# Attention scores of a hybrid decoder on Trainium2: one product over 128 rows in place of two heads side by side on 64 rows

## The chip, the core and the metric

The kernel runs on one core of one Trainium2 chip, as one launch. The metric is the device time of one launch in microseconds. The core has a matrix engine (PE, with its weight loads shown as PEld), a vector engine (DVE), a scalar engine (ACT), a general engine (POOL) and a queue engine (SP) that issues nearly all transfers. Each engine works through its own instructions in the order in which they stand, and waits on semaphores for the others.

## What is computed

The reference is a decoder trunk of two layers on 512 tokens of width 1024: the first layer mixes tokens by forgetting attention with 16 heads of 64, the second by a short gated convolution, and each is followed by a squared-ReLU MLP and a gated embedding. The change is in the attention of the first layer, whose core is:

```python
q = q * HEAD_DIM ** -0.5                       # 16 heads of 64
c = cumsum(log_sigmoid(f_logit))               # per head and token
s = einsum('bhqd,bhkd->bhqk', qb, k)           # per block of 128 queries
s = s + cb[..., :, None] - c[..., None, :]
s = where(k_pos <= q_pos, s, NEG_INF)
pr = softmax(s)
o = einsum('bhqk,bhkd->bhqd', pr, v)
return o @ w_out
```

All arrays are float32. The kernel multiplies in a rounded float32 form (fp32r in the profile): each operand is split into a high part, which is the rounded value, and a low part, which is the rest, and a product is made of three: high by high, low by high, high by low.

## The kernel before, in words

**Stages.** `attention` (L336) norms the tokens, projects the values (tiles `v`), and then runs three kinds of work interleaved. `project(i)` (L418) makes q and k of the two heads 2i and 2i+1 as one 128-row page each: rows 0 to 63 belong to the first head, rows 64 to 127 to the second. It takes 48 products of 512 columns (tiles `qk`, L214 to L216), first for k, then for q, and a split into high (ACT, L222 and L432) and low (DVE, L223 and L433) after each. `scores(i, b)` (L459) multiplies query block b of both heads with the keys up to that block, in tiles `sc`, and does the softmax on DVE (L474, L479), ACT (L478) and POOL (L480), on pages `prr`, `pr` and `prl` into which `bias(h)` (L441) has loaded the decay terms (`neg_c`) by four transfers for each head. `turn(h, j)` (L484) transposes the weights (tiles `pT`) and splits them into `ph` and `pl`; `mix(h, j)` (L498) multiplies them with the values (tiles `ps_o`).

**The products of the scores.** For one block the kernel issues three products for each head (L466 to L470): q.hi by k.hi, q.hi by k.lo and q.lo by k.hi. Each contracts over the 64 rows of one head. The two heads' products alternate in the text of the program; a scheduler may move them apart.

**The order of the work.** A loop over steps c (L611) places the interleaved work: scores run 12 steps ahead of `turn` (`SCORED`), `mix` runs 2 behind it (`LAG`), and a generator `stream` (L548) supplies filler for PE: first the steps of `project(1)` to `project(7)`, three products each, 112 steps in all, then parts of the output projection (tiles `o`). A number of steps, `share + AHEAD`, says how many filler steps are done by step c (L615 to L621); `AHEAD` is 2. The tile framework's scheduler then moves instructions within that order. Weights arrive by transfers into 14 `raw` pages (L119), are split into `wh` (ACT, L222) and `wl` (DVE, L223), and everything else lives on 70 pages of 128 by 512. All of the kernel's loads, the decay terms and the weights among them, are issued by SP in one order.

Of the kernel before, what the change touches and what calls it, by code (L numbers as in the profile page):

```python
# [8 lines left out]
F32 = mybir.dt.float32  # L9
# [16 lines left out]
PUT_OFF = 46000  # L26
LAG = 2
AHEAD = 2
PAGES = 70
RAWS = 14  # L30
LEAD = 1
# [32 lines left out]
def trunk(ctx: ExitStack, tc, x, pT, g, wv, wqk, bf, wo, wci, cw, wco, wup, wdn, wpp, wpg, out):  # L64
# [13 lines left out]
    def bank(name):  # L78
        return psum.tile([P, S], F32, tag="ps", name=name)
# [256 lines left out]
    def attention(hT, first_x, g0, by_hand):  # L336
# [78 lines left out]

        stacked, probs, outs, both = {}, {}, {}, {}

        def project(i):  # L418

            q, key = (Pair(page(f"{n}h{i}", F32R), page(f"{n}l{i}", F32R)) for n in "qk")  # L420
            stacked[i] = q, key
            for s in (1, 0):
                ps = bank(f"qk{i}_{s}")
                for k in range(KT):
                    mm3(
                        ps, narrow("qk", i, k=k, c=s * P),
                        hT.at(lambda h: h[:, k, :]), k == 0, k == KT - 1,
                    )
                    if k < KT - 1:
                        yield  # L430
                if s == 0:
                    nc.scalar.mul(q.hi[:, :S], ps, HD**-0.5)  # L432
                    nc.vector.scalar_tensor_tensor(  # L433
                        out=q.lo[:, :S], in0=ps, scalar=HD**-0.5, in1=q.hi[:, :S].bitcast(F32),
                        op0=ALU.mult, op1=ALU.subtract,
                    )
# [22 lines left out]
        def scores(i, b):  # L459


            q, key = stacked[i]
            n = (b + 1) * P
            nm = max(n, 256)
            heads = [(2 * i + e, slice(64 * e, 64 * e + 64), bank(f"sc{2 * i + e}_{b}")) for e in range(2)]
            for s, (at, to) in enumerate(((q.hi, key.hi), (q.hi, key.lo), (q.lo, key.hi))):  # L466
                for _, r, ps in heads:
                    nc.tensor.matmul(  # L468
                        ps[:, :nm], at[r, b * P : n], to[r, :nm], start=s == 0, stop=s == 2
                    )  # L470
            for h, _, ps in heads:
# [139 lines left out]
        for c in range(-SCORED, n_sc + LAG):  # L611
# [350 lines left out]
```

## Time and profile before

| | |
|---|---|
| median of 3 runs | 1263.35 us (1263.23 to 1263.46) |
| span of the profiled execution, first to last instruction | 1262.1 us |
| PE busy in the span | 1238.7 us (98%) |
| DVE, ACT, POOL busy | 906.1, 604.0, 627.5 us |
| stretch with scores in it | 82.0 to 227.6 us |

The profiled execution has no time of its own beside its span, so the span stands for it: it lies 1.25 us under the median. In rows of the timeline, the columns are start, duration, engine, line, operation, output and inputs, and the number of instructions merged into the row; two heads' products that start together are merged as x2. Matmuls are pipelined and their ends modelled, so what one product costs is read from the distance between two starts and not from its duration. In rows of windows, each engine has its busy microseconds and its instructions. A stage is read from its own window: the share over the whole span mixes stages.

### The profile page before, as it was taken

The numbers are of one execution on the slowest core, as the hardware profiler recorded it, in microseconds if no ns is written. First come the engines' busy times: TensorE is split into PE (matmuls) and PEld (weight loads), VectorE is DVE, ScalarE is ACT, GpSimd is POOL, SyncE is SP. The second block draws the span as 40 slices with busy tenths as digits, with TensorE's granted clock in tenths as the row PEclk, the third lists the DMA queues.
The fourth block names the chain that finished last, engine by engine and source line by source line (L and its number), as shares of the span: only waits on it lengthen the run. The fifth ranks groups of instructions, "written<-read, shape, count | busy, mean of one in ns | idle before, by whom it ended". The sixth has DMA issues, their size and how long they took to land.

```text
span 1262.1 us, 18000 instructions
## 1 busy us (share of the span) xinstructions
PE 1238.7 (98%) x6036; PEld 1022.3 (81%) x6036; DVE 906.1 (72%) x1386; ACT 604.0 (48%) x1293; POOL 627.5 (50%) x631
## 2 busy tenths in 40 slices
PE   7999999999999999999999999999999999999997
PEld 6877777788888888888789988889788888888876
DVE  5645666767788788879867444457778897779973
ACT  5445656654645434554455333344653445535451
POOL 2027555328787777876211000016777777878210
PEclk9999999999999999999999999999999999999999
DMA  7554342161432244227333233432323442235401
GB/s 249 152 142 149 100 126 76 62 224 65 134 95 86 87 134 134 84 68 258 126 100 94 74 101 101 141 124 86 94 74 101 134 130 84 71 117 175 159 18 50
DMA packets 83228, 144.48 MB, mean 114 GB/s; under 512 B 9600, under 2 KB 16816, under 8 KB 83136
## 3 DMA queue, kind: packets, MB, share of 16 engines
q1 hardware_dynamic: 82928, 143.07, 36.3%
q8 instruction: 47, 0.77, 0.2%
q14 instruction: 45, 0.37, 0.1%
q10 hardware_dynamic: 144, 0.26, 0.1%
q0 software_dynamic: 64, 0.00, 0.0%
HBM read 136.93 MB, written 6.37 MB: 114 GB/s over the span
## 4 chain that ended last, share of the span: by engine, by line
PE 60%; DVE 18%; POOL 7%; issue 6%; ACT 6%; DMA 3%; SPq 1%; DVEq 0%; POOLq 0%; ACTq 0%
DVE wl L223 10%; POOL s L720 4%; PE up L215 3%; PE up L216 3%; PE up L214 3%; ACT wh L222 3%; PE dn L215 3%; PE qk L214 3%; PE dn L216 3%; PE dn L214 3%; DVE acc L752 2%; PE qk L216 2%; PE qk L215 2%; PE sc L468 2%; PE pg L214 2%
## 5 line engine op out<-in xcount | busy, mean ns | idle before, releaser
L223 DVE TENSOR_TENSOR wl<-raw,wh 128x512 fp32r<-128x512 f32 (+1 forms) x404 | 365.2, 955 | 25.3 <-ACT wh L222 24.6
L222 ACT CAST wh<-raw 128x512 fp32r<-128x512 f32 (+1 forms) x404 | 219.5, 619 | 8.9 <-DVE xd L296 5.0
L215 PE MATMUL up<-hTh,wl 128*128 128x512 f32 (+1 forms) x576 | 210.5, 366 | 0.0
L216 PE MATMUL up<-hTl,wh 128*128 128x512 f32 (+1 forms) x576 | 210.0, 366 | 0.0
L214 PE MATMUL up<-hTh,wh 128*128 128x512 f32 (+1 forms) x576 | 209.7, 366 | 0.0
L223 POOL TENSOR_TENSOR wl<-T,wh 128x512 fp32r<-128x512 f32 x112 | 160.9, 1468 | 35.8 <-ACT wh L222 32.0
L215 PEld LDWEIGHTS up<-hTh,wl 128*128 128x128 f32 x576 | 108.7, 189 | 17.6
L214 PEld LDWEIGHTS up<-hTh,wh 128*128 128x128 f32 x576 | 108.6, 189 | 17.5
L216 PEld LDWEIGHTS up<-hTl,wh 128*128 128x128 f32 x576 | 108.3, 189 | 17.3
L752 DVE TENSOR_TENSOR acc<-dn,acc 128x512 f32<-128x512 f32 x168 | 107.4, 679 | 10.5 <-PE dn L216 10.5
L131 POOL TENSOR_TENSOR T<-raw,raw 128x512 f32<-128x512 f32 x56 | 87.5, 1573 | 37.0 <-DMA raw<-in_wdn 24.8
L706 ACT ACTIVATE r<-up 128x512 f32<-128x512 f32 (+1 forms) x72 | 38.7, 547 | 126.3 <-PE up L216 126.3
L131 POOL TENSOR_TENSOR T<-raw,T 128x512 f32<-128x512 f32 x56 | 91.3, 1631 | 2.2
L692 DVE TENSOR_TENSOR q<-r 128x512 f32<-128x512 f32 (+1 forms) x72 | 66.9, 936 | 29.2 <-ACT r L706 29.2
L237 POOL TENSOR_SCALAR cor_r_v<-cos,cos 128x1 f32<-128x1 f32 x4 | 1.6, 398 | 159.1 <-ACT junk L245 159.1
L222 ACT CAST wh<-T 128x512 fp32r<-128x512 f32 x112 | 61.2, 617 | 0.0
L222 ACT CAST A11h<-q 128x256 fp32r<-128x256 f32 x28 | 11.4, 407 | 99.9 <-DVE q L692 99.9
L214 PE MATMUL pg<-wh,hTh 128*128 128x512 f32 x128 | 50.9, 398 | 3.4 <-ACT hTh L222 3.3
L214 PE MATMUL qk<-hTh,wh 128*128 128x512 f32 x128 | 53.0, 414 | 0.0
L759 POOL TENSOR_TENSOR acc<-acc,acc 128x512 f32<-128x512 f32 x28 | 47.0, 1708 | 10.0 <-DVE acc L752 10.0
L216 PE MATMUL qk<-hTl,wh 128*128 128x512 f32 x128 | 50.8, 397 | 0.0
L215 PE MATMUL qk<-hTh,wl 128*128 128x512 f32 x128 | 50.5, 395 | 0.0
(236 smaller groups left out, 3067.1 us busy)
## 6 DMA issues: line engine op xcount, KB each, us to landing
raw<-in_wup SPq DMA_DIRECT2D x128, 256.0 KB, 2.9
raw<-in_wdn SPq DMA_DIRECT2D x128, 256.0 KB, 2.8
raw<-in_wci SPq DMA_DIRECT2D x48, 256.0 KB, 3.5
raw<-in_wqk SPq DMA_DIRECT2D x32, 256.0 KB, 3.8
raw<-in_wpg SPq DMA_DIRECT2D x32, 256.0 KB, 3.8
g<-in_g SPq DMA_DIRECT2D x22, 256.0 KB, 5.4
prl<-neg_c SPq DMA_DIRECT2D x16, 256.0 KB, 6.7
raw<-in_wo SPq DMA_DIRECT2D x16, 256.0 KB, 2.7
```

The costliest lines, as they stand in the source:

```text
L131: nc.gpsimd.tensor_tensor(out=B[name, p], in0=B[a, p], in1=B[b, p], op=ALU.subtract)
L214: nc.tensor.matmul(ps, a.hi, b.hi, start=start, stop=False)
L215: nc.tensor.matmul(ps, a.lo, b.hi, start=False, stop=False)
L216: nc.tensor.matmul(ps, a.hi, b.lo, start=False, stop=stop)
L222: nc.scalar.copy(hi, src)
L223: eng.tensor_tensor(out=lo, in0=src, in1=hi.bitcast(F32), op=ALU.subtract)
L468: nc.tensor.matmul(ps[:, :nm], at[r, b * P : n], to[r, :nm], start=s == 0, stop=s == 2)
L692: nc.vector.tensor_tensor(out=out, in0=r, in1=r, op=ALU.mult)
L706: nc.scalar.activation(r[:, :n], ps[:, :n], AF.Relu)
L720: sums = lambda out, a, b, op: nc.gpsimd.tensor_tensor(out=out, in0=a, in1=b, op=op)
L752: nc.vector.tensor_tensor(out=a, in0=banks[s], in1=a, op=ALU.add)
L759: nc.gpsimd.tensor_tensor(out=a, in0=a, in1=acc[i, s][:, :S], op=ALU.add)
```

## The change

Each head gets its high and low parts one above the other, so that one product over 128 rows sums two of the three. For the first head of a pair, the rows of q.hi become (high of q, low of q) and a new page pair `k0` holds (high of k, high of k) and (low of k, low of k); for the second head a new page `q1` holds (high of q, low of q), and the old k pages become (high, high) and (low, low). The new sum also holds low by low, which the three products left out. Getting there takes nine transfers inside SBUF for each pair of heads, each of 64 rows by 512, issued by SP (`place`): six after the split of k and three after that of q. Some overwrite rows that an earlier one of them reads, and wait for it. `scores` then issues two products for each head, over all 128 rows, in place of three over 64. Three more pages are held for each pair. The filler is done sooner: `STACK` lets `project` run 12 steps ahead of `share` and not 2, until its 112 steps are done; the output projection's steps keep the old rule.

```diff
+STACK = 12
...
+        def place(out, to, src, of):
+            nc.sync.dma_start(out[to, :S].bitcast(F32), src[of, :S].bitcast(F32))
...
-            stacked[i] = q, key
+            low, high = slice(0, HD), slice(HD, P)
...
+                    q1 = page(f"q1_{i}", F32R)
+                    place(q1, low, q.hi, high)
+                    place(q1, high, q.lo, high)
+                    place(q.hi, high, q.lo, low)
                 else:
                     split(key.hi[:, :S], key.lo[:, :S], ps)
+                    k0 = Pair(*(page(f"k0{s}{i}", F32R) for s in "hl"))
+                    for of, to in ((key.hi, k0.hi), (key.lo, k0.lo)):
+                        place(to, low, of, low)
+                        place(to, high, of, low)
+                        place(of, low, of, high)
                 yield
+            stacked[i] = (q.hi, k0), (q1, key)
...
-            heads = [(2 * i + e, slice(64 * e, 64 * e + 64), bank(f"sc{2 * i + e}_{b}")) for e in range(2)]
-            for s, (at, to) in enumerate(((q.hi, key.hi), (q.hi, key.lo), (q.lo, key.hi))):
-                for _, r, ps in heads:
+            heads = [(2 * i + e, bank(f"sc{2 * i + e}_{b}")) for e in range(2)]
+            for (h, ps), (at, key) in zip(heads, stacked[i]):
+                for s, to in enumerate((key.hi, key.lo)):
                     nc.tensor.matmul(
-                        ps[:, :nm], at[r, b * P : n], to[r, :nm], start=s == 0, stop=s == 2
+                        ps[:, :nm], at[:, b * P : n], to[:, :nm], start=s == 0, stop=s == 1
                     )
...
-            while done < share + AHEAD:
+            while done < max(share + AHEAD, min(share + STACK, 112)):
```

PE's order, at block 2 of heads 8 and 9 (`sc8_2`, `sc9_2`), before; `qh`, `ql`, `kh` and `kl` are the high and low parts of q and k, and each score product is one head's, over 64 rows:

```order
L468 MATMUL sc8_2_2176<-kh4_1686,qh4_1684 128x384
L468 MATMUL sc8_2_2176<-kl4_1687,qh4_1684 128x384
L468 MATMUL sc8_2_2176<-kh4_1686,ql4_1685 128x384
L216 MATMUL qk5_0_2142<-hTl_84,wh42_1460 128x512
L214 MATMUL qk5_0_2142<-hTh_83,wh42_1460 128x512
L215 MATMUL qk5_0_2142<-hTh_83,wl42_1461 128x512
L216 MATMUL qk5_0_2142<-hTl_84,wh42_1460 128x512
L214 MATMUL qk5_0_2142<-hTh_83,wh43_1504 128x512
L468 MATMUL sc9_2_2177<-kh4_1686,qh4_1684 128x384
L468 MATMUL sc9_2_2177<-kl4_1687,qh4_1684 128x384
L509 MATMUL ps_o5_2117<-ph5_2_2113,v2_1_141 128x256
L468 MATMUL sc9_2_2177<-kh4_1686,ql4_1685 128x384
```

The same block now; `k0h`, `k0l` and `q1` are the new pages, and each product is over 128 rows:

```order
L482 MATMUL sc8_2_2267<-k0h4_1719,qh4_1575 128x384
L482 MATMUL sc8_2_2267<-k0l4_1720,qh4_1575 128x384
L217 MATMUL qk6_1_2179<-hTl_84,wh47_1705 128x512
L482 MATMUL sc9_2_2268<-kh4_1577,q1_4_1839 128x384
L482 MATMUL sc9_2_2268<-kl4_1578,q1_4_1839 128x384
L523 MATMUL ps_o5_2199<-ph5_2_2195,v2_1_141 128x256
L524 MATMUL ps_o5_2199<-pl5_2_2196,v2_1_141 128x256
```

The scheduler had moved the two heads' products apart in both; there were six over 64 rows, and there are four over 128. In the whole program the score products stood in 45 stretches between other work and now stand in 41.

PE's order around block 1 of heads 12 and 13 (`sc12_1`, `sc13_1`), before:

```order
L487 MATMUL pT9_2_2702<-ident_75,prr9_1903 128x128
L487 MATMUL pT9_2_2702<-ident_75,prl9_1902 128x128
L509 MATMUL ps_o9_2709<-ph9_0_2616,v0_2_134 128x512
L510 MATMUL ps_o9_2709<-pl9_0_2617,v0_2_134 128x512
L468 MATMUL sc12_1_2712<-kh6_2278,qh6_2276 128x256
L468 MATMUL sc12_1_2712<-kl6_2279,qh6_2276 128x256
L468 MATMUL sc13_1_2713<-kh6_2278,qh6_2276 128x256
L468 MATMUL sc13_1_2713<-kl6_2279,qh6_2276 128x256
L468 MATMUL sc12_1_2712<-kh6_2278,ql6_2277 128x256
L468 MATMUL sc13_1_2713<-kh6_2278,ql6_2277 128x256
L214 MATMUL qk7_0_2734<-hTh_83,wh48_1985 128x512
L215 MATMUL qk7_0_2734<-hTh_83,wl48_1986 128x512
```

And now, at the same place:

```order
L501 MATMUL pT9_2_2775<-ident_75,prr9_1988 128x128
L501 MATMUL pT9_2_2775<-ident_75,prl9_1987 128x128
L524 MATMUL ps_o8_2654<-pl8_3_2687,v3_2_146 128x256
L523 MATMUL ps_o9_2782<-ph9_0_2705,v0_2_134 128x512
L524 MATMUL ps_o9_2782<-pl9_0_2706,v0_2_134 128x512
L482 MATMUL sc12_1_2785<-k0h6_2319,qh6_2175 128x256
L482 MATMUL sc12_1_2785<-k0l6_2320,qh6_2175 128x256
L523 MATMUL ps_o9_2782<-ph9_1_2747,v1_2_138 128x384
L482 MATMUL sc13_1_2786<-kh6_2177,q1_6_2439 128x256
L482 MATMUL sc13_1_2786<-kl6_2178,q1_6_2439 128x256
L501 MATMUL pT9_3_2805<-ident_75,prl9_1987 128x128
L524 MATMUL ps_o9_2782<-pl9_1_2748,v1_2_138 128x384
```

The filler (`qk7`) has left this place. Between the first transpose of head 9 (`pT9_0`) and the first product of the output projection (`o0_0`) there stood 36 filler products of 512 columns; now there is none, since they stand earlier.

SP's order of transfers at the second pair of heads, before; `raw` are weights, `prr`, `pr` and `prl` the decay terms of a head:

```order
L119 DMA raw48_1987<-in_wqk 128x512
L119 DMA raw49_2009<-in_wqk 128x512
L453 DMA prr2_1025<-neg_c_151 128x128
L453 DMA pr1_1023<-neg_c_151 128x256
L453 DMA prr2_1025<-neg_c_151 128x384
L453 DMA prl2_1024<-neg_c_151 128x512
L453 DMA prr3_1100<-neg_c_151 128x128
L453 DMA pr1_1023<-neg_c_151 128x256
L453 DMA prr3_1100<-neg_c_151 128x384
L453 DMA prl3_1099<-neg_c_151 128x512
L119 DMA raw50_2054<-in_wqk 128x512
L453 DMA prr4_1218<-neg_c_151 128x128
```

And now, at the same place:

```order
L421 DMA k0h1_1013<-kh1_960 64x512 x2
L421 DMA k0l1_1014<-kl1_961 64x512 x2
L421 DMA kh1_960<-kh1_960 64x512
L421 DMA kl1_961<-kl1_961 64x512
L421 DMA q1_1_1068<-qh1_958 64x512
L468 DMA prr2_1074<-neg_c_151 128x128
L421 DMA q1_1_1068<-ql1_959 64x512
L421 DMA qh1_958<-ql1_959 64x512
L468 DMA pr1_1072<-neg_c_151 128x256
L468 DMA prr2_1074<-neg_c_151 128x384
L468 DMA prl2_1073<-neg_c_151 128x512
L468 DMA pr1_1072<-neg_c_151 128x256
```

The nine transfers of a pair stand ahead of the decay terms of the next heads (`prr2`, `pr1`, `prl2`), and some of each follow one another in one queue.

More of the change, by code (lines that the diff above doesn't have):

```diff
@@ L459, in scores @@
         def scores(i, b):
-            q, key = stacked[i]
             n = (b + 1) * P
             nm = max(n, 256)
-            heads = [(2 * i + e, slice(64 * e, 64 * e + 64), bank(f"sc{2 * i + e}_{b}")) for e in range(2)]
-            for s, (at, to) in enumerate(((q.hi, key.hi), (q.hi, key.lo), (q.lo, key.hi))):
-                for _, r, ps in heads:
+            heads = [(2 * i + e, bank(f"sc{2 * i + e}_{b}")) for e in range(2)]
+            for (h, ps), (at, key) in zip(heads, stacked[i]):
+                for s, to in enumerate((key.hi, key.lo)):
                     nc.tensor.matmul(
-                        ps[:, :nm], at[r, b * P : n], to[r, :nm], start=s == 0, stop=s == 2
+                        ps[:, :nm], at[:, b * P : n], to[:, :nm], start=s == 0, stop=s == 1
                     )
-            for h, _, ps in heads:
+            for h, ps in heads:
                 pr = probs[h][b]
```

## The prediction

> **What bounds the kernel now.** I read the page first, then the waits of PE, the chain, and the windows and timeline of the stretch with scores.
>
> ```profile
> span 1262.1 us, 18000 instructions
> PE 1238.7 (98%) x6036; PEld 1022.3 (81%) x6036; DVE 906.1 (72%) x1386; ACT 604.0 (48%) x1293; POOL 627.5 (50%) x631
> ```
>
> PE is busy 98% of the span, the next engine 72%. In the windows of the attention (columns: stretch, its length, then busy us and instructions of PE, PEld, DVE, ACT, POOL, the clock, and transfers) PE is never idle until 227 us, at full clock:
>
> ```profile
> 82.00:194.20 112.20, 112.20 (x581) 82.92 (x581) 71.60 (x221) 67.98 (x174) 67.41 (x113) 1.00 0.42 122
> 194.20:212.10 17.90, 17.90 (x94) 13.00 (x92) 12.40 (x36) 12.53 (x32) 11.33 (x20) 1.00 0.38 128
> 212.10:217.00 4.90, 4.90 (x24) 4.05 (x24) 2.84 (x8) 1.94 (x6) 3.13 (x2) 1.00 0.01 3
> 217.00:227.00 10.00, 10.00 (x59) 7.50 (x58) 6.24 (x22) 5.85 (x17) 3.49 (x7) 1.00 0.00 0
> 227.00:232.00 5.00, 4.91 (x29) 3.65 (x30) 4.90 (x13) 4.74 (x13) 2.37 (x3) 1.00 0.17 60
> 232.00:238.00 6.00, 6.00 (x28) 4.57 (x27) 4.79 (x12) 3.71 (x10) 4.28 (x9) 1.00 0.35 119
> ```
>
> But a busy PE is not one that streams without gaps. The timeline of PE at one block of 512 keys, both heads together:
>
> ```profile
> 89.00 0.39 PE L215 MATMUL qk<-hTh,wl 128*128 128x512 f32 x1
> 89.22 0.39 PE L216 MATMUL qk<-hTl,wh 128*128 128x512 f32 x1
> 89.54 0.50 PE L468 MATMUL sc<-kh,qh 64*128 64x512 f32 x2
> 89.88 0.40 PE L468 MATMUL sc<-kl,qh 64*128 64x512 f32 x2
> 90.11 0.39 PE L468 MATMUL sc<-kh,ql 64*128 64x512 f32 x2
> 90.44 0.50 PE L214 MATMUL qk<-hTh,wh 128*128 128x512 f32 x1
> 90.77 0.40 PE L215 MATMUL qk<-hTh,wl 128*128 128x512 f32 x1
> ```
>
> A product of 512 columns takes 0.23 us from start to start (about 0.2275 over a long run), and two heads on 64 rows each share one slot. From 89.22 to 90.77 there are five slots, 1.14 us, and 1.55 us pass. So 0.41 us are lost at one visit to the 64-row form: 0.09 ahead of the first score product, and 0.10 to 0.11 behind it, behind the last and behind the first product after. A block whose heads stand apart pays that twice, and its slots hold one head each:
>
> ```profile
> 121.54 0.39 PE L215 MATMUL qk<-hTh,wl 128*128 128x512 f32 x1
> 121.86 0.44 PE L468 MATMUL sc<-kh,qh 64*128 64x384 f32 x1
> 122.14 0.33 PE L468 MATMUL sc<-kl,qh 64*128 64x384 f32 x1
> 122.31 0.34 PE L468 MATMUL sc<-kh,ql 64*128 64x384 f32 x1
> 122.58 0.50 PE L216 MATMUL qk<-hTl,wh 128*128 128x512 f32 x1
> 122.92 0.40 PE L214 MATMUL qk<-hTh,wh 128*128 128x512 f32 x1
> ```
>
> Here 1.38 us pass for two slots of 0.2275 and three of 0.17: again 0.41 lost. A different operand alone costs nothing: among 128-row products the trace goes from `qk` to `ps_o` and back at the usual distances, 0.23 and 0.17:
>
> ```profile
> 130.01 0.40 PE L216 MATMUL qk<-hTl,wh 128*128 128x512 f32 x1
> 130.24 0.34 PE L509 MATMUL ps_o<-ph,v 128*128 128x384 f32 x1
> 130.41 0.39 PE L214 MATMUL qk<-hTh,wh 128*128 128x512 f32 x1
> ```
>
> The loss belongs to the change of row form. The Trainium skill, page TensorEngine Tiling (Array Packing), section Key Properties, says the same: a change of tiling mode drains the engine. It gives no price; the rows above do.
>
> **The change, part by part.** *Visits removed.* By the order the 192 score products stand in 45 stretches between other work. At 0.41 us each that is 18.5 us; the total would be less only if some visit were free, and none in the timeline is, so I hold 17 to 20 us possible and take 19.
>
> *Slots.* Blocks by width, from the counts of one of the three products, of which each block has two:
>
> ```profile
> L468 PE MATMUL sc<-kh,qh x64: 275/411/502, 82.0 to 227.0; 64*128 64x256 f32 x32, 64*128 64x384 f32 x16, 64*128 64x512 f32 x16
> ```
>
> That is 16 blocks of 256, 8 of 384, 8 of 512. The price of 256 columns over 128 rows is 0.12 us:
>
> ```profile
> 62.11 0.28 PE L215 MATMUL v<-wh,hTl 128*128 128x256 f32 x1
> 62.23 0.28 PE L216 MATMUL v<-wl,hTh 128*128 128x256 f32 x1
> 62.35 0.28 PE L214 MATMUL v<-wh,hTh 128*128 128x256 f32 x1
> ```
>
> Now each block takes four slots: 64 x 0.12 + 32 x 0.17 + 32 x 0.2275 = 20.4 us. Before, a block took three slots with its heads together and six with them apart; by the timeline 14, 2 and 6 blocks of the three widths are together, one of 256 takes four slots and the rest six, so 52 x 0.115 + 42 x 0.17 + 30 x 0.2275 = 19.9 us. The slots cost 0.5 us more. PE's work falls by 19 - 0.5 = 18.5 us.
>
> At this point a rule speaks against the change. The Trainium skill, the same page, section Theoretical Speedup, gives a contraction of at most 64 rows up to twice the speed by two row tiles at once, which the change gives up. By that rule alone, with all 32 blocks together and no visit paid, the kernel would become 5 us slower (a fourth slot for each block, 16 x 0.12 + 8 x 0.17 + 8 x 0.23). The x2 rows agree with it for the slots, and the 0.41 us beside them is what it leaves out.
>
> *Filler moved.* The 36 filler products that stood between `pT9_0` and `o0_0` (8.2 us) now stand earlier; PE's work in sum is the same. Their cover is gone from the stretch 194.2 to 212.1. PE's own work left there is 17.9 - 8.2 - 2.5 (six visits) = 7.2 us, and DVE has 12.4 us there now. If all of DVE's work stayed there and bound, PE would lose 5.2 us; if the scores, which run 12 steps ahead, and the weight splits that leave with the filler free enough of DVE, nothing. By the new order two weight splits, some 1.4 us, leave the stretch, and the output projection's first products follow to absorb a rest. I take 2.5, between the ends.
>
> *The thinner tail.* From 217 to 238 six visits and some slots go, about 2.7 us, of 21. DVE is busy 15.9 us there, but 4.90 of 5.00 between 227 and 232, where a faster PE finds it late. Bounds 0 and 2.7 us lost; I take 1, since 217 to 227 has room (6.2 us of DVE in what would be 7.7).
>
> *Transfers.* 72 are added, nine for each pair, of 64 rows by 2 KB, 128 KB each. No row shows one inside SBUF. The nearest are (issue, count, size, median us from issue to landing):
>
> ```profile
> raw<-in_wqk SPq DMA_DIRECT2D x32, 256.0 KB, 3.8
> prl<-neg_c SPq DMA_DIRECT2D x16, 256.0 KB, 6.7
> pr<-neg_c SPq DMA_DIRECT2D x16, 128.0 KB, 5.9
> kept<-xb SPq DMA_DIRECT2D x8, 256.0 KB, 2.2
> ```
>
> A copy out of SBUF lands in 2.2 us at twice the size, decay terms in 5.9 to 6.7 because ten are issued at once. I take 2.5, and 6.7 as the upper end. The last step of a pair is two landings deep: `q1` must land before the rows of `qh` under it are overwritten. Before that come the last product and the split of q:
>
> ```profile
> 126.82 0.40 PE L216 MATMUL qk<-hTl,wh 128*128 128x512 f32 x1
> 127.58 0.60 ACT L432 ACTIVATE qh<-qk 128x512 fp32r<-128x512 f32 x1
> 128.31 0.69 DVE L433 SCALAR_TENSOR_TENSOR ql<-qk,qh 128x512 fp32r<-128x512 f32 x1
> ```
>
> From the product's start to the end of the split: 2.2 us. So a pair is ready after 2.2 + 2 x 2.5, some 7.5 us with issue. By the order, PE has this much other work between the last product of q and the first score: 9.7 us at the first pair, 11.7 at the second, 14.8 at the third, 18 at the next four, 12 at the last. The step `STACK` buys that, and the transfers are covered by projection products. What is queued behind a waiting transfer on SP: the next decay terms, for which POOL and then DVE wait, and weights, which are split two pairs ahead of use. Three more pages per pair also make some `k0` wait for a page that PE frees some 3 us later. I charge 0.5 us, with ends at 0 and, from the longer landing, 18 us (second rival). A gain from the transfers themselves is excluded: nothing waited for less.
>
> Sum: 18.5 - 2.5 - 1 - 0.5 = 14.5 us. The other stages keep their order and PE bounds them, so the gain should stay. The span of 1262.1 becomes 1247.6, and the time, which lies 1.25 us over the span, 1248.9.
>
> **The rivals.** *First: DVE takes over in both thin stretches.* Everything at its upper end, 5.2 and 2.7 us, and waits from `pT` through ACT and DVE to `ps_o` at each of the six steps without filler, 0.6 us each, would leave 18.5 - 5.2 - 2.7 - 3.6 = 7 us: 1256.4. For it: 4.90 of 5.00. Against: 71.6 of 112.2 before. Chance 0.11.
>
> *Second: the transfers land late.* At 6.7 us each a pair is ready after 2.2 + 13.4 + about 1 for issue, 16.6 us, and the scores wait 6.9, 4.9, 1.8 and 4.6 us at the first, second, third and last pair, 18.2 in all: 18.5 - 18.2 - 3.5 is 3.2 us slower, 1266.6. At 5.9 each the waits are 5.3, 3.3, 0.2 and 3.0, and 3.2 us are gained, 1260.2. Its middle is 1263. It begins at landings of 3.3 us. For it: ten decay terms share the queue. Against it: the new transfers stand ahead of them. Chance 0.08: 0.03 faster, 0.03 within the measurement, 0.02 slower.
>
> *Third, on the other side: the loss is not the row form's.* If the 0.41 us belongs to each new run of scores (their accumulation begins, their weights load anew), it stays at the 41 stretches that the order now has. Four fewer save 1.6 us, the slots cost 0.5 and the other losses 4: 2.9 us slower, 1266.3. It decides where a visit still costs more than 0.34 us (18.5 - 41 x 0.34 = 4.5). Against it: 0.23 and 0.17 around `ps_o`, which also begins accumulations with new weights. Chance 0.06.
>
> **How the numbers follow.** The forecast, with losses between nothing and 8 us, has 0.75: gains of 10 to 19 us. The predicted time is 1248.9. The range takes in the first rival and all of the visits: 1243.5 to 1256.4, and leaves out the other two and a little of the forecast's ends. A measurement of this kernel can tell 0.2%, 2.5 us, from no change. Faster: 0.75 + 0.11 + 0.03 = 0.89; same 0.03; slower 0.06 + 0.02 = 0.08.
>
> **What would show it right or wrong.** In the profile after, score rows should read 128x256 to 128x512 and stand 0.12, 0.17 and 0.23 us apart, with no row of `qk` late behind them; a distance of 0.3 there means the third rival. The waits of PE should show `sc` or `qk` behind transfers for under 1 us in sum; several us at the first two pairs are the second. Between `pT9_0` and `o0_0` waits of `ps_o` for `pl` of some 2.5 us are expected; over 5, with DVE full, are the first. The prediction is wrong if PE's time from the first score to the last falls by less than 10 us.

## The result: slower, 1278.49 us against 1263.29

| kernel | median us | range us | ratio to the kernel before, 95% interval |
|---|---|---|---|
| before | 1263.29 | 1263.18 to 1263.46 | |
| changed | 1278.49 | 1275.94 to 1280.22 | 1.0118 [1.0106, 1.0130] |

The change costs 15.2 us where 14.5 were to be gained. The profiled execution took 1278.0 us, its span is 1276.3.

```profile
span 1276.3 us, 18024 instructions
PE 1230.1 (96%) x5972; PEld 1028.0 (81%) x5972; DVE 906.2 (71%) x1386; ACT 602.2 (47%) x1293; POOL 631.1 (49%) x631
```

PE's busy time has fallen by 8.6 us, from 1238.7, and its idle time has risen from 23.4 us (1262.1 - 1238.7) to 46.2. Nearly all of that lies in the attention: the windows from the first score product to the last product of `ps_o` (columns as in the prediction), before and after:

```profile
82.00:247.00 165.00, 164.23 (x855) 122.51 (x855) 108.39 (x321) 101.82 (x259) 92.02 (x152) 1.00 0.35 105
```

```profile
85.00:260.00 175.00, 152.42 (x773) 126.36 (x772) 104.88 (x320) 98.00 (x256) 93.61 (x152) 0.94 0.49 142
```

PE is busy 12 us less in this stage, 4 of them because some 18 filler products now stand ahead of it, and stands idle for 22.6 us where it stood for 0.8. The granted clock is 0.94 in place of 1.00, and the DMA engines are busy 0.49 of the time in place of 0.35. What PE waits for is nearly one thing, by the waits of PE (total, times, longest):

```profile
PE ps_o L523 <- POOL ph L508: 20.8, 7, 7.6
```

`ph` at L508 is the short zero fill of a probability page, 0.2 us of POOL's work. PE's timeline shows the new score products, and then the longest such wait:

```profile
113.01 0.39 PE L482 MATMUL sc<-k0h,qh 128*128 128x512 f32 x1
113.24 0.39 PE L482 MATMUL sc<-k0l,qh 128*128 128x512 f32 x1
113.46 0.39 PE L482 MATMUL sc<-kh,q 128*128 128x512 f32 x1
113.69 0.39 PE L482 MATMUL sc<-kl,q 128*128 128x512 f32 x1
113.92 0.39 PE L217 MATMUL qk<-hTl,wh 128*128 128x512 f32 x1
...
116.91 0.27 PE L501 MATMUL pT<-ident,prl 128*128 128x128 f32 x1
124.82 0.58 PE L523 MATMUL ps_o<-ph,v 128*128 128x256 f32 x1 [7.64 <-POOL ph L508]
125.20 0.41 PE L524 MATMUL ps_o<-pl,v 128*128 128x256 f32 x1
125.41 0.63 PE L215 MATMUL qk<-hTh,wh 128*128 128x512 f32 x1
125.84 0.63 PE L216 MATMUL qk<-hTh,wl 128*128 128x512 f32 x1
```

The scores and the `qk` behind them stand 0.23 us apart: the loss at each visit is gone, as forecast. Behind the wait products of 512 columns stand 0.43 us apart, and do so until 129.9.

Why the fill is late is read one engine back. POOL's timeline of the same time:

```profile
115.36 0.29 POOL L469 TENSOR_SCALAR_AFFINE_SELECT pr<-pr 128x128 f32<-128x128 f32 x1 [2.74 <-DMA pr<-neg_c]
...
118.94 0.29 POOL L469 TENSOR_SCALAR_AFFINE_SELECT prl<-prl 128x128 f32<-128x128 f32 x1 [1.51 <-DMA prl<-neg_c]
...
123.10 0.29 POOL L469 TENSOR_SCALAR_AFFINE_SELECT prr<-prr 128x128 f32<-128x128 f32 x1 [0.86 <-DMA prr<-neg_c]
124.33 0.29 POOL L469 TENSOR_SCALAR_AFFINE_SELECT prl<-prl 128x128 f32<-128x128 f32 x1 [0.93 <-DMA prl<-neg_c]
124.56 0.21 POOL L508 MEMSET ph<- 128x128 f32 x1
```

POOL works its row in order, and the fill stands behind masks (L469) of the next pair's decay terms, whose loads have not landed. From 80 to 250 us POOL waits 60.8 us for such loads at its masks; before it was 24.9. One step further back is SP, which issues those loads. Its timeline before:

```profile
93.87 0.38 SPq L453 DMA_DIRECT2D prr<-neg_c  x1
...
99.52 1.92 SPq L453 DMA_DIRECT2D prr<-neg_c  x2
101.53 0.38 SPq L453 DMA_DIRECT2D prl<-neg_c  x1
```

And after, the same two heads' decay terms (scores began 3 us later here):

```profile
98.29 1.35 SPq L421 DMA_DIRECT2D k0h<-kh  x2
99.75 1.17 SPq L421 DMA_DIRECT2D k0l<-kl  x2
105.56 0.46 SPq L421 DMA_DIRECT2D kh<-kh  x1
...
107.90 0.58 SPq L468 DMA_DIRECT2D prr<-neg_c  x1
108.53 0.46 SPq L421 DMA_DIRECT2D q<-ql  x1
111.06 0.46 SPq L421 DMA_DIRECT2D qh<-ql  x1
...
114.73 1.96 SPq L468 DMA_DIRECT2D prr<-neg_c  x2
116.78 0.38 SPq L468 DMA_DIRECT2D prl<-neg_c  x1
```

The decay terms are issued at 107.90 and 114.73 instead of 93.87 and 99.52. Ahead of them and among them SP issues nine transfers at about half a microsecond each, and stands still twice: from 100.9 to 105.56 until the two copies out of `kh` have landed, which the transfer into `kh` would overwrite, and from 109.0 to 111.06 likewise for q. SP's waits from 80 to 250 us (total, times, longest), and the landings from 70 to 250:

```profile
SPq L421 <- DMA k0h<-kh: 22.6, 7, 4.7
SPq L421 <- DMA q<-qh: 9.3, 7, 2.2
```

```profile
k0h<-kh SPq DMA_DIRECT2D x16, 128.0 KB, 6.1
q<-qh SPq DMA_DIRECT2D x8, 128.0 KB, 2.3
```

The copies of q land in 2.3 us. The copies out of k into `k0`, issued behind loads, take 6.1 and 5.1. The decay terms are issued late and do not land late: from issue to landing they take 4.9 to 7.0 us (median of each size), before 5.0 to 6.7.

### The profile page after: what moved, and what is told of

It is laid out like the page before. It is cut to its first block, busy times and chain, and to the rows that moved or that the text cites. A ratio compares the mean times of both kernels' runs of the same rounds, so it can differ in the third digit from the quotient of the medians.

```text
span 1276.3 us, 18024 instructions
## 1 busy us (share of the span) xinstructions
PE 1230.1 (96%) x5972; PEld 1028.0 (81%) x5972; DVE 906.2 (71%) x1386; ACT 602.2 (47%) x1293; POOL 631.1 (49%) x631
## 4 chain that ended last, share of the span: by engine, by line
PE 69%; DVE 12%; DMA 5%; issue 4%; ACT 4%; POOL 4%; SPq 1%; DVEq 0%; POOLq 0%; ACTq 0%
PE up L217 6%; PE up L216 6%; PE up L215 6%; DVE wl L224 5%; PE dn L216 5%; PE dn L215 5%; PE dn L217 5%; PE pg L215 2%; PE pg L217 2%; PE pg L216 2%; PE qk L215 2%; PE qk L216 2%; PE qk L217 2%; ACT junk L246 2%; DVE n_h L254 1%
## 5 line engine op out<-in xcount | busy, mean ns | idle before, releaser
L469 POOL TENSOR_SCALAR_AFFINE_SELECT prr<-prr 128x128 f32<-128x128 f32 x32 | 11.1, 352 | 82.0 <-DMA prr<-neg_c 48.6
```

## The experiments

Three theories were on record first. **Theory 1:** SP waits for landings at the overwriting transfers, so that decay terms are issued late; POOL stands at their masks, its zero fills come late, and PE's `ps_o` waits. **Theory 2:** the added bytes make every transfer land late, whoever waits. **Theory 3:** the stretch left without filler by `STACK` is what costs the time. All times are medians beside 1263.3 to 1263.6 for the kernel before in the same sets of runs. Where a run leaves the stacking out of the result, so that its output is not the reference's, its entry says so.

### The terms of the forecast, apart

**No transfers.** The 128-row products read q's and k's pages as they are, so the stacking is left out of the result:

```diff
-                    q1 = page(f"q1_{i}", F32R)
-                    place(q1, low, q.hi, high)
...
-            stacked[i] = (q.hi, k0), (q1, key)
+            stacked[i] = (q.hi, key), (q.hi, key)
```

> The 128-row products and the earlier filler stay; the nine transfers and the three new pages of each pair are left out, so both heads multiply the pages as they are and the scores of the two heads are summed. Theory 1 (SP waits for landings of transfers that overwrite rows, issues the next decay terms late, and POOL's masks and the memsets behind them hold up ps_o) and theory 2 (the added bytes make everything land late) both say that the 34 us of gaps on PE go: 1244 to 1250 us, with no wait of ps_o for POOL over 0.5 us. Theory 3 (the stretch without filler costs the time) says over 1255 us, with gaps behind pT9.

Measured 1249.09 us, ratio 0.9887 [0.9872, 0.9902]. The window of the stage:

```profile
85.00:231.00 146.00, 144.01 (x774) 121.36 (x773) 107.41 (x320) 97.55 (x256) 92.11 (x152) 1.00 0.38 114
```

PE is idle for 2 us here, and for 22.6 in the changed kernel. Products, tail and earlier filler together come out at 14.2 us of gain; so the nine transfers, with the three pages that they fill, cost 1278.49 - 1249.09 = 29.4 us. Theory 3 is out.

**Earlier filler alone**, in the kernel before:

```diff
+STACK = 12
...
-            while done < share + AHEAD:
+            while done < max(share + AHEAD, min(share + STACK, 112)):
```

> The kernel before with the rule for the earlier filler alone (STACK = 12), old products, no transfers. Theories 1 and 2: 1263 to 1267 us, since DVE works while PE has no filler. Theory 3: over 1272 us.

Measured 1268.85, ratio 1.0044 [1.0027, 1.0061]: 5.5 us. That isn't the price of the missing filler alone, since the order of the old products changed with it. PE's timeline shows 49 visits to the 64-row form in place of 45, and more heads apart. Counted from the starts, with the prediction's prices for 256, 384 and 512 columns, the visits lose 20.1 us in place of 18.5 and the score products' slots take 23.2 in place of 19.9: 4.9 of the 5.5 us. So 1268.85 - 1249.09 = 19.8 us isn't what the products gain over the kernel before. The same count for the run without transfers gives 1.1 us lost around its 43 stretches of scores and 20.1 in slots. By PE's rows the products thus gain 18.5 + 19.9 - 1.1 - 20.1 = 17.2 us over the kernel before, and 3.0 of them are lost again to the moved filler and the tail, which leaves the 14.2.

**The transfers and the filler with the old products** (64 rows, six to a block; the transfers' results go unused or overwrite halves that the products read, so the result is not the reference's):

```diff
-            stacked[i] = (q.hi, k0), (q1, key)
+            stacked[i] = q, key
...
```

> The transfers and the earlier filler stay; the products are the old ones, three for each head over 64 rows, on pages that the transfers have partly overwritten, so the scores differ. Theories 1 and 2: the visits to the 64-row form come back and the gaps stay, so 1278.5 + 19 = 1290 to 1299 us if both costs are separate; less, down to 1280, if the slower PE gives the transfers time. Theory 3: about 1264 us.

Measured 1277.38, ratio 1.0108 [1.0093, 1.0123], less than expected, and the same as the changed kernel. With nine transfers some 17 us or more of PE's work make no difference: PE no longer sets the pace of this stage.

### What of the transfers costs

**Six instead of nine**, those that overwrite left out (so the pages keep halves of their own there, and the scores are not the reference's):

```diff
-                    place(q.hi, high, q.lo, low)
...
-                        place(of, low, of, high)
```

> Of the nine transfers the three that overwrite rows read by an earlier one (kh, kl and qh onto themselves or from ql) are left out, so SP never waits for one of them to land; six of nine remain, and the scores differ. Theory 1: most of the 34 us of gaps go, 1247 to 1256 us. Theory 2: two thirds of the bytes remain, so a third of the gaps goes, about 1267 us.

Measured 1257.4, ratio 0.9961 [0.9948, 0.9974]: 21 of the 29.4 us come back. It takes three transfers away along with SP's waits, so it does not say which of the two it is. It holds the same three pages more for each pair as the change, so these pages and six whole transfers together cost 1257.40 - 1249.09 = 8.3 us.

**Twelve, each to a fresh page**, none overwriting, all of the computation kept:

```diff
-                        place(to, low, of, low)
-                        place(to, high, of, low)
-                        place(of, low, of, high)
+                        for u, half in zip(to, (low, high)):
+                            place(u, low, of, half)
+                            place(u, high, of, half)
...
```

> The changed kernel with every half copied to a fresh page: twelve transfers a pair instead of nine, six fresh pages instead of three, none written over what another transfer reads, so SP never waits at L421 for a landing; a third more bytes move inside SBUF. Theory 1 (SP's wait for landings) expects 1256 to 1263: the 1257.4 of the six without the overwriting three, and up to 6 us for six more transfers to issue and land. Theory 2 (bytes) expects it no better than the changed kernel, 1278 or more.

Measured 1278.78, ratio 1.0118 [1.0103, 1.0133]. SP's waits for landings at overwriting transfers are gone and the time is what it was, so Theory 1 in its first form doesn't explain this kernel. The run also adds three transfers and three pages, so it doesn't show that the waits cost nothing with nine. SP's timeline shows what stands there now:

```profile
102.36 1.21 SPq L421 DMA_DIRECT2D k0h<-kh  x2
103.67 1.90 SPq L421 DMA_DIRECT2D k1h<-kh  x2
105.96 1.82 SPq L421 DMA_DIRECT2D k0l<-kl  x2
108.54 1.58 SPq L421 DMA_DIRECT2D k1l<-kl  x2
110.22 0.54 SPq L421 DMA_DIRECT2D q<-qh  x1
...
112.78 0.54 SPq L471 DMA_DIRECT2D prr<-neg_c  x1
```

From 102.36 to 112.70 SP is at these twelve, some 4 us of it in short waits that end with work on other tiles, as when a page comes free. The decay terms come after it, at 112.78.

**An eighth of the bytes**, same issues, order and waits; the products read the pages as in the first run, so the stacking is left out:

```diff
-            nc.sync.dma_start(out[to, :S].bitcast(F32), src[of, :S].bitcast(F32))
+            nc.sync.dma_start(out[to, :64].bitcast(F32), src[of, :64].bitcast(F32))
...
```

> Nine transfers a pair with the same issues on SP, the same order and the same waits for landings, but each moves only 64 of 512 columns, an eighth of the bytes; the 128-row products read the pages of q and k as they are, so the stacking is left out of the result. Theory 1 in the form that the twelve fresh transfers leave it (what SP spends on the transfers, issuing each for about 0.5 us and waiting for landings, is what holds the decay terms back) expects 1268 to 1278. Theory 2 (the bytes fill the DMA engines) expects 1250 to 1256, near the 1249.1 without transfers. In between, the landings that SP waits for have become shorter with the bytes, and both count.

Measured 1264.97, ratio 1.0008 [0.9998, 1.0017]: between the two theories. Small transfers still cost 1264.97 - 1249.09 = 15.9 us, and 13.5 go with the other seven eighths of the bytes.

**The same without waits for landings**: the narrow run with the overwriting transfers sent to pages that nothing reads.

```diff
-                    place(q.hi, high, q.lo, low)
+                    place(page(f"q2_{i}", F32R), high, q.lo, low)
...
```

> The narrow run with its three overwriting transfers sent to pages of their own that nothing reads: nine issues a pair of an eighth of the bytes, and no wait at SP for a landing. The stacking is left out of the result as in the narrow run. If SP's waits for landings are what the narrow run's 16 us over no transfers were (1264.97 against 1249.09), it falls to 1249 to 1253; if the nine issues are, it stays at 1261 to 1266; between them, both.

Measured 1262.46, ratio 0.9990 [0.9981, 0.9999]. Without the waits 2.5 of the 15.9 us are gone; 13.4 are left to nine issues a pair, and to the six more pages that they take, which this run doesn't tell apart. These prices don't add up freely: six whole transfers, without waits and with three more pages, cost 8.3, less than nine small ones.

### Which link carries it

**Zero fills on DVE** instead of POOL, the computation whole:

```diff
-                    nc.gpsimd.memset(z[:, lo_q : j * P].bitcast(F32), 0.0)
+                    nc.vector.memset(z[:, lo_q : j * P].bitcast(F32), 0.0)
```

> The changed kernel, whole, with one edit: the 32 short zero fills of ph and pl (L508) are DVE's instead of POOL's, so they no longer stand in POOL's row behind masks whose decay term has not landed. This tries the last link of theory 1. If the fill is how the late decay terms reach PE, the waits of ps_o for POOL's ph (20.8 us by the page) go and the time falls to 1255 to 1262, near the 1257.4 that leaving out the in-place transfers gave. If the masks themselves hold PE, through the score rows and the transposes, the waits move to sc or pT and the time stays at 1272 or above. Between them, both count.

Measured 1273.18, ratio 1.0075 [1.0059, 1.0090]: 5.3 us come back. The waits on POOL's fill are gone, and others stand in their place:

```profile
PE pT L501 <- POOL prl L494: 6.3, 4, 2.3
...
PE ps_o L523 <- DVE pl L508: 4.7, 1, 4.7
```

**Masks later in POOL's row**, three visits of the loop after the loads, with POOL's row in the program's order:

```diff
+        pool_row.enter_context(tc.manual_schedule(engines={E.Pool}))
...
+                if c == 8 * (h // 2) - SCORED - (4 if h % 2 == 0 else 1):
+                    masks(h)
```

> The changed kernel with POOL's row written out in the program's order and each head's masks three visits of the loop (some 8 us) after its decay terms' loads; SP's row, all nine transfers and all loads stay. If POOL's standing at masks, with work for the earlier heads behind them in its row, is how the late decay terms reach PE, its waits at L474 fall from 61 us to under 25 and the time to 1255 to 1265. If the masks only move the same wait to another place, or PE's loss comes by another way (weights or transfers landing late), it stays at 1272 or above.

Measured 1273.36, ratio 1.0073 [1.0058, 1.0088]. POOL's waits at the masks from 80 to 250 us, first in the changed kernel, then here:

```profile
POOL prr L469 <- DMA prr<-neg_c: 44.7, 17, 7.3
...
POOL pr L469 <- DMA pr<-neg_c: 9.4, 8, 2.7
POOL prl L469 <- DMA prl<-neg_c: 6.7, 7, 1.5
```

```profile
POOL prr L474 <- DMA prr<-neg_c: 10.6, 8, 2.3
POOL prl L474 <- DMA prl<-neg_c: 9.5, 9, 1.5
POOL pr L474 <- DMA pr<-neg_c: 4.3, 2, 3.3
```

The first half of the expectation holds: 60.8 us became 24.4, about what the kernel before has. The second doesn't: the time falls by 5 us, not 13 or more. The wait that the profile names is real, and taking it away gives back 5 of the 29 us; PE then waits for something else. Here that is some 16.5 us in many small waits, the longest sort 3.5 us at `qk` for a bank that DVE frees.

**Decay terms issued by ACT** instead of SP, the computation whole:

```diff
-                nc.sync.dma_start(pr, neg_c[b, h : h + 1, :n].partition_broadcast(P))
+                nc.scalar.dma_start(pr, neg_c[b, h : h + 1, :n].partition_broadcast(P))
```

> The changed kernel, whole, with the decay terms' loads (L468) issued by ACT instead of SP: all nine transfers and all the bytes remain, and SP still waits for the landings at L421, but no decay term stands behind that wait. Theory 1 (SP's row) expects ps_o's waits for POOL to fall under 8 us in all and the time to be 1254 to 1262, as long as ACT itself does not stand at a load whose page is not free. Theory 2 (the added bytes make every transfer land late, whoever issues it) expects 1270 or more with the waits of POOL's masks for prr as long as in the changed kernel (44.7 us between 80 and 250).

Measured 1268.39 (1261.28 to 1274.79 in ten runs), ratio 1.0030 [1.0007, 1.0053]: some 10 us come back, between the theories. The profiled execution is the fastest of the ten, 1261.28 us with all nine transfers. `ps_o` waits 3.5 us for POOL in it, as Theory 1 expects, and POOL waits 37.3 us for decay terms at its masks. The spread of 13.5 us is itself a change; its cause is open.

**The same with twelve fresh transfers**, the computation whole:

```diff
-                        place(to, low, of, low)
-                        place(to, high, of, low)
-                        place(of, low, of, high)
+                        for u, half in zip(to, (low, high)):
+                            place(u, low, of, half)
+                            place(u, high, of, half)
...
-                nc.sync.dma_start(pr, neg_c[b, h : h + 1, :n].partition_broadcast(P))
+                nc.scalar.dma_start(pr, neg_c[b, h : h + 1, :n].partition_broadcast(P))
```

> The twelve transfers to fresh pages, with no waits for landings, and the decay terms' loads issued by ACT. SP issued for 103 of the 160 us from 80 to 240 with twelve; without the decay terms that is some 74. If SP's row (issues ahead of the decay terms) is what makes twelve as slow as nine, 1255 to 1264. If the bytes in the DMA engines are, which stay the same, 1272 or above. ACT then waits at its own loads where a page is not free; 7 us of that were seen with the decay terms on ACT before, and they are in the range.

Measured 1280.80, ratio 1.0131 [1.0116, 1.0146]: nothing comes back. That looks like the second theory (other queue, same bytes, same time), but two readings of the traces speak against it. ACT's row issues the decay terms of heads 4 and 5 at 106.70 to 115.69 us, where SP issued them at 112.78 to 119.35 with twelve transfers and at 107.90 to 116.78 in the changed kernel. So they are 4 to 6 us earlier, yet about as late as in the changed kernel, and the run doesn't separate their lateness from the bytes. And once issued they land in 3.7 to 6.9 us (median of each size), about as soon as before, 5.0 to 6.7. The Trainium skill, page DMA: Bandwidth & Descriptors, section Issuing engines are not separate DMA queues, has issuing from another engine save the issue time alone, as all share the same DMA engines; no run here settles that.

**Decay terms four visits earlier**, ahead of the pair's last transfers, the computation whole:

```diff
-                if c == 8 * (h // 2) - SCORED - (7 if h % 2 == 0 else 4):
+                if c == max(8 * (h // 2) - SCORED - (11 if h % 2 == 0 else 8), -SCORED):
```

> The changed kernel, whole, with each head's decay terms and their masks put four visits of the loop earlier, about 6 us of PE's work, so that they stand ahead of the pair's last transfers in SP's row. If the decay terms' place behind the transfers is the cause, POOL's masks are in time and it falls to 1256 to 1266. If SP has too much to issue in all, or the pages are not free earlier, the same lateness comes back at another place and it stays at 1273 or above.

Measured 1288.56, ratio 1.0191 [1.0175, 1.0206]: worse by 10. Now q's transfers stand behind the decay terms' bytes; SP's waits over the whole launch, and the landing:

```profile
SPq L421 <- DMA q<-qh: 29.2, 8, 4.8
```

```profile
q<-qh SPq DMA_DIRECT2D x8, 128.0 KB, 6.5
```

The copies of q that stand behind the decay terms land late: 2.3 us became 6.5, and SP's waits there, over the whole launch, went from 9.6 to 29.2. The decay terms themselves land in 4.6 to 5.8 us, where they took 4.9 to 7.0. Nor are they all earlier: heads 4 and 5 have theirs issued from 107.26 to 111.47 us.

**The old order of filler** with nine transfers, the computation whole:

```diff
-STACK = 12
+STACK = 2
```

> The changed kernel, whole, with the filler's order of the kernel before (STACK 2 instead of 12). The earlier filler alone cost 5.5 us. If that sum holds beside the transfers, 1272 to 1274; but the transfers then have some 4 us less of PE's work to land in, so if the scores now wait for their pair, PE waits at sc and it is 1278 or above.

Measured 1282.32, ratio 1.0151 [1.0133, 1.0169]. Now it is the scores that wait for their pair, by PE's waits:

```profile
PE sc L482 <- DMA qh<-ql: 13.7, 5, 5.0
```

So the step `STACK` did its own work in the changed kernel: there no wait of `sc` for a transfer is among PE's waits above 1 us. The wait that the forecast's second rival names, of the scores for their pair, is found in this run and not in the changed kernel.

### Versions without the transfers, or with fewer

All of these compute the reference.

**Direct writes:** ACT and DVE write each 64-row part from PSUM to the half where it is wanted.

```diff
+                    for key, a, b in zip(keys, (low, high), (high, low)):
+                        split(key.hi[a, :S], key.lo[a, :S], ps[a, :])
+                        nc.scalar.copy(key.hi[b, :S], ps[a, :])
...
```

> The 128-row score products with no transfers at all: ACT and DVE write each 64-row part from PSUM straight to the half where it is wanted, across the halves where needed (q's stack of the second head has low over high, which changes no sum). Filler order as in the changed kernel. It costs 4 more ACT instructions (about 0.58 us) and 4 more DVE instructions (about 0.69 us) a pair, 19 and 22 us over the eight pairs; DVE then is busy some 131 of the 160 us from 80 to 240. Theory 1 and the terms of the forecast without its transfers expect 1250 to 1256 (1249.1 without the stacking, and up to 7 for DVE's and ACT's longer rows). If DVE takes over there, 1258 or more, with PE waiting for DVE's pl, nmx or the scores.

Measured 1260.70, ratio 0.9977 [0.9968, 0.9987]: faster than before, and 11.6 over the run without transfers. DVE is busy 124.8 us in the stage in place of 107.4.

And with the old order of filler:

```diff
-STACK = 12
+STACK = 2
```

> The 128-row products with no transfers, each part written by ACT and DVE to the half where it is wanted (as in the run before), now with the filler's order of the kernel before. If the earlier filler costs its 5.5 us here too, 1254 to 1257, which beats both kernels. If the scores then wait for the last parts of q, which DVE writes in two instructions, or DVE's 22 us more are what costs, 1259 or above.

Measured 1257.35, ratio 0.9948 [0.9933, 0.9963], just past the upper end of the first case. With 128-row products the earlier filler thus costs some 3.4 us (1260.70 - 1257.35), near the 3.0 found above.

**Four transfers a pair**, for the second copy of k alone, the rest written directly, `STACK` 2:

```diff
-                        nc.scalar.copy(key.hi[b, :S], ps[a, :])
...
+                        place(key.hi, b, key.hi, a)
+                        place(key.lo, b, key.lo, a)
```

> The 128-row products with four transfers a pair: ACT and DVE write q's four parts and the first copy of k's parts each to its half, and transfers of 64 rows fill only the other half of k's four pages; none overwrites what another reads. Filler's order of the kernel before. Against the run with no transfers and STACK 2 (1257.4) it takes two ACT and two DVE instructions off each pair, 20 us of the 41, and adds about 2 us of SP's issuing a pair. If the count of transfers on SP decides, 1248 to 1255. If any transfers ahead of the decay terms cost, 1258 to 1264.

Measured 1257.97, ratio 0.9962 [0.9948, 0.9976]; the 20 us of ACT's and DVE's instructions taken off bought nothing that shows. Either four transfers cost about what those did, or neither costs much here.

With more time to land:

```diff
-STACK = 2
+STACK = 6
```

> As the run before, with the filler six steps ahead instead of two, so that k's transfers have some 5 us more to land. If the scores wait for those transfers with STACK 2, this is the faster, 1249 to 1254; if they do not, it costs part of the 3 to 5 us that earlier filler has cost, 1251 to 1258.

Measured 1257.42, ratio 0.9947 [0.9932, 0.9962]: no difference to `STACK` 2.

And four transfers with the masks later in POOL's row:

```diff
+        pool_row.enter_context(tc.manual_schedule(engines={E.Pool}))
...
+                if c == 8 * (h // 2) - SCORED - (4 if h % 2 == 0 else 1):
+                    masks(h)
```

> The kernel with four transfers a pair (1257.97), with the same edit of POOL's row. There PE waited 6.4 us for POOL's zero fills and 1.3 us for its products, and POOL some 36 us at masks. If that standing is the cause, 1248 to 1254; if not, 1256 or above.

Measured 1255.66, ratio 0.9936 [0.9919, 0.9952]: the fastest whole kernel of the study, 7.7 us under the kernel before; its interval meets that of the direct writes. It falls short of the 1248 to 1254 expected, so POOL's row is here too a small part. POOL no longer waits for a `prr` load here, and PE's longest sort of wait from 80 to 250 us is 2.5 us.

### The stage in eleven of them

From the first score product to the last of `ps_o`, from the windows (the kernel before and the last two, which have the old order of filler, have some 18 products more in it):

| kernel | stage us | PE busy | idle | clock | DMA share |
|---|---|---|---|---|---|
| before | 164.9 | 164.1 | 0.8 | 1.00 | 0.35 |
| no transfers | 145.5 | 143.5 | 2.0 | 1.00 | 0.38 |
| six transfers | 154.8 | 145.9 | 8.9 | 0.99 | 0.48 |
| nine narrow, no waits | 159.8 | 151.5 | 8.3 | 0.99 | 0.38 |
| nine narrow | 161.6 | 148.4 | 13.2 | 0.98 | 0.38 |
| nine (the change) | 174.9 | 152.3 | 22.6 | 0.94 | 0.49 |
| nine, old products | 175.7 | 168.0 | 7.7 | 0.97 | 0.49 |
| twelve, fresh pages | 175.5 | 157.0 | 18.5 | 0.94 | 0.57 |
| twelve, decay terms on ACT | 176.5 | 159.8 | 16.7 | 0.94 | 0.56 |
| direct, `STACK` 2 | 157.2 | 151.8 | 5.4 | 0.99 | 0.38 |
| four, masks later | 156.4 | 150.5 | 5.9 | 0.99 | 0.63 |

The mean share of the DMA engines doesn't order these kernels: the last row has the largest, 0.63, and the fastest time.

## Why the prediction was wrong

The prediction set itself a test: PE's time from the first score to the last was to fall by 10 us or more. It grew by 10, from 145.6 us (82.0 to 227.6) to 155.5 (85.1 to 240.6). By its steps:

**Visits removed: right.** 18.5 us were forecast with the slots; PE's rows give 17.2 (the old visits cost 18.5 by themselves, as forecast, and 1.1 stays around the new ones). The slots' 0.5 us uses 0.12 us for 256 columns now and 0.115 before; with one price it is 0.1 to 0.2. The score rows stand 0.12 to 0.23 us apart in the profile after. The third rival, that the loss isn't the row form's, is out.

**Filler moved and thinner tail: about right.** 2.5 and 1 us were taken; together 3.0 are left by PE's rows, and neither was measured by itself. The 5.5 us of the filler alone with the old products are mostly the 64-row form's. Without the transfers the sum is 18.5 - 2.5 - 1 = 15.0 us; 14.2 were measured.

**Transfers: the step that failed.** "I charge 0.5 us, with ends at 0 and, from the longer landing, 18 us." They cost 29.4. The step asked whether a pair lands before its scores need it, and there its answer holds: PE hardly waits for a pair. The landing of 2.5 us holds for q (2.3) and not for the copies out of k (6.1 and 5.1), which stand behind loads. The text named who is queued behind a waiting transfer on SP, "the next decay terms, for which POOL and then DVE wait, and weights", and gave that queue no price. What it needed was at hand: 72 issues on SP, decay terms that took 5 to 6.7 us to land among themselves before (eight loads for two heads by SP's rows, not ten at once), and POOL's row in order behind them. What the runs showed in its place: the decay terms (of heads 4 and 5, say) are issued some 11 to 12 us later, measured from the first score, and PE stands idle for 22.6 us and runs slowly after the long waits. The second rival counted only the scores' wait, and its 1260 to 1267 comes by a way that the change doesn't take.

**What is shown, and what stays open.** Shown: the transfers, with their pages, are the cause, since 29.4 us come back without them and the products gain about what was forecast. With nine as the change has them, or twelve, the stage takes 175 to 177 us with the new products, and with nine 176 with the old. Taken away in one order, the 29.4 are 13.5 us with seven eighths of the bytes, 2.5 with the waits for small landings, and 13.4 with the nine issues and their pages; but six whole transfers with three more pages cost 8.3 in all, so the parts are not prices that hold by themselves. Not settled: by which chain this reaches PE. The wait that the profile of the changed kernel names, POOL's fill behind masks, gives 5 us when it is taken away by either of two edits, and then other waits take its place. Late landing of the decay terms isn't it, since they land about as soon after their issue as before. The mean share of the DMA engines isn't it by itself, as the fastest whole kernel has the largest. The pool of pages, from which each pair now takes three to six more, wasn't tried apart: three more cost 8.3 us at most together with six transfers, but for nine or twelve transfers SP, ACT and POOL each show some microseconds of waits that end with work on a tile that isn't their source, as when a page comes free. Lateness of the decay terms remains a candidate: no run issued them as early as before while it kept all nine transfers. And the order of PE's own row differs between these kernels, so a few microseconds between any two of them may be that.

## What to carry to other kernels

Price a transfer by what stands behind it in the same queue too, and not only by whether its own reader can wait: count what one loop's period of the issuing engine holds (here some 20 us a pair, of which nine transfers take 5 to issue and 4.6 in waits), and look at who is next in it. A transfer that overwrites what another reads makes the queue stand until that one has landed (4.7 us at the longest here). Giving it a page bought nothing here, 1278.78 us with twelve; letting the engine that produces the data write it to its place did, 1260.70. And a wait that tops the profile is tested before it is believed: here taking it away gave 5 of 29 us.

## What the runs showed of the hardware

**An idle PE comes back slow.** After the wait of 7.64 us products of 512 columns stood 0.43 us apart instead of 0.23, for 5.1 us, from 124.82 to 129.9. The granted clock over these 5.1 us is 0.51, and 1.00 over the next four. That costs 5.1 x (1 - 0.23/0.43), by estimate some 2.4 us beyond the wait itself. Over the stage, PE's busy time is 152.4 us with nine transfers and 144.0 without for the same products, 8.4 us on top of 20.6 us more of idle time. The Trainium skill, page TensorE: Matmul & The Clock Gate, section Part 1: The HAM clock gate (the "warmup" mystery), gives half the clock after at least one idle window of some 3.4 us, and the whole clock after at least one such window of sustained work. The halving agrees, and the slow stretch of 5.1 us fits with that "at least".

**Half the rows take as long.** In the version with direct writes, by the groups of instructions (count, busy us, mean ns):

```profile
L439 ACT ACTIVATE q<-qk 64x512 fp32r<-64x512 f32 x14 | 8.3, 593 | 4.2 <-DVE q L440 3.9 <-PE qk L217 0.2
L440 DVE SCALAR_TENSOR_TENSOR q<-qk,q 64x512 fp32r<-64x512 f32 x14 | 9.6, 688 | 1.8 <-ACT q L439 1.1
```

The split of all 128 rows of q took 600 and 690 ns by the prediction's rows: writing in halves doubles the time of these instructions. How much of the direct version's 11.6 us over no transfers that is was not shown.

**Nine to twelve small instructions on a queue engine are not small.** Issuing a transfer of 64 rows occupied SP for 0.46 us and up to 1.6, most for 0.5, whether 2 KB or 256 bytes a row: nine narrow ones a pair without a wait for landings still cost 13.4 us with their pages.
